# A Mamba-2 and MoBA trunk: the SSD inputs turned on VectorE, four head pairs to a visit, and an output block split in two

## The chip, the core and the metric

The kernel runs on one NeuronCore of one Trainium2 chip. The metric is the device time of one execution in microseconds; the time before is 1143.02 us, the median of three runs (1142.99 to 1146.43).

## What is computed

x is 256 tokens of 2048 float32 channels. A Mamba-2 layer with 64 heads of 64 channels in 8 groups is followed by an attention layer and a last RMSNorm. The change lies in the Mamba-2 layer:

```python
proj = h @ w_in                                   # z, xbc, dt
xbc = silu(causal_depthwise_conv(xbc, conv_w, conv_b))
dt = softplus(dt + dt_bias); a = dt * -exp(A_log)
x_dt = xs * dt[..., None]                         # xs: 8 groups x 8 heads x 64 channels
a_cum = cumsum(a); decay = exp(where(causal, a_cum[l] - a_cum[s], -inf))
cb = einsum("blgn,bsgn->blsg", cm, bm)
y = einsum("bsgrl,bsgrp->blgrp", cb * decay, x_dt)  # one chunk of 256 tokens: the state is zero
y = y + D_skip * xs
y = grouped_rmsnorm(y * silu(z), gnorm_g, 8)
x = x + y @ w_out                                 # 4096 rows of w_out, 512 to a group
```

## The kernel before

**The stream of products.** Nearly all of TensorE's work is weight matrices times activations. Each matrix is read as blocks of 512 columns; a *unit* is 256 rows of such a block. SyncE loads a unit into a `raw` buffer (512 KB, four of them), ScalarE rounds it to `hi`, VectorE makes the remainder `lo`, and TensorE does twelve products of 128x512 into two PSUM banks `ps` (two halves of the tokens, two slices of 128 rows, and hi, hi, lo). `hi` and `lo` have five buffers each, and the program writes the split of unit u+3 ahead of the products of unit u.

**The order of blocks** is the string ORDER: B and C are the columns of `bm` and `cm`, d those of dt, x0 to x7 and z0 to z7 the groups of `xs` and of the gate. o0 to o3 are four column blocks of `w_out` over groups 0 and 1, o10 to o13 the same columns over groups 2 and 3, p0 to p3 over groups 4 to 7 (eight units each). After them come the attention layer's matrices.

**Turning a block.** A finished block has tokens on the partitions and is wanted with channels there. `turn` has VectorE transpose 32x32 pieces into `T`, SyncE write `T` to DRAM (`turned`), and GpSimd's queue read it back in four pieces into `U`, in another order of the pieces.

**The side work.** The rest of the layer is written as generators, whose steps the program puts between the unit's products: `some` takes a step when a clock of its own, kept from costs for each instruction and DMA (LOAD, WRITE, READ), says that its inputs are there. That fixes each engine's order at build time; engines execute in that order and wait for data. For a group g these are:
- `conv_gen`: convolution and SiLU, giving `xs` (channels on the partitions). For x blocks it then transposes `xs` back on TensorE, two visits of four 128x128 transposes into a bank `s`; after each, VectorE multiplies by dt into `xd` (tokens on the partitions).
- `pair_gen`, four per group, one per pair of heads: loads the cumulated decay into `em` (two buffers), ScalarE and VectorE make `cb * decay`. Every second one then does the products of `xd` and `em` for two pairs, one bank for each, and VectorE adds the D term into `yt` and multiplies with the gate z.
- `norm_gen`: grouped RMSNorm, giving the operand `yn` of the o and p blocks.

All compute instructions have line 126 in the profile (a helper issues them), so rows are told apart by tile names.

Of the kernel before, what the change touches and what calls it, by code (L numbers as in the profile page):

```python
# [9 lines left out]
F32 = mybir.dt.float32  # L10
# [23 lines left out]
ORDER = "B0 d0 C0 x0 z0 x1 z1 x2 z2 x3 z3 B1 o0 C1 o1 x4 o2 z4 x5 o3 z5 x6 o10 z6 x7 o11 z7 o12 o13 p0 p1 p2 p3".split()  # L34
# [135 lines left out]
def trunk_kernel(ctx: ExitStack, tc: tile.TileContext, x, a_norm_g, a_w_in, a_conv_w, a_conv_b,  # L170
# [31 lines left out]
    def dram(t, offset, ap):  # L202
# [9 lines left out]
    S = [Slots(work, {"T": ([P, 512], 2), "u": ([P, 4, L], 1), "xs": ([P, 4, L], 3), "xd": ([P, 2, 512], 1),  # L212
                      "cb": ([P, 384], 4), "em": ([P, 2, 384], 2), "z": ([P, 1024], 1), "yt": ([P, 4, L], 2)})]
# [58 lines left out]
    def lay_out():  # L272
        for b in blocks:
            ks = b["ks"][::16 if b["form"] == "dt" else 2]
            if b["form"] == "rows":
                units.extend([(b, k, None) for k in ks[:3]] + [(b, k, j) for j in (0, 1) for k in ks[3:]])
            else:
                units.extend((b, k, None) for k in ks)

        def late(first, n, m):  # L280

            i = next(i for i, u in enumerate(units) if u[0] is first)
            p, q = units[i:i + n], units[i + n:i + 2 * n]
            units[i:i + 2 * n] = p[:n - m] + q[:n - m] + p[n - m:] + q[n - m:]

        late(blocks[n_out], 8, 2)
        late(blocks[n_fin], 8, 2)
# [121 lines left out]
    ga = const.tile([16, P], F32, name="ga")  # L409
# [90 lines left out]
    r0 = nt[:, 2, :]  # L500

# [6 lines left out]
    def first_norm():  # L508
        DVE.tensor_reduce(nt[:, 0, :], ss, axis=mybir.AxisListType.X, op=OP.add)
        root(nt, D)  # L510

# [65 lines left out]
    def dt_gen(w):  # L577
# [38 lines left out]
        dal = const.tile([P, 2, P], F32, name="dal", tag="c2")  # L616
# [4 lines left out]
    def conv_gen(U, there, c, key, group=None):  # L621
# [20 lines left out]
        give(u)  # L642
        st[key], when[key] = v, clock.last
        if group is None:
            return
        yield lambda: "dal" in st and can("xd")()
        xd = take("xd")
        for i in (0, 2):
            yield can("s")
            p = take("s").rearrange("p (t c) -> p t c", t=2)  # L650
            for e in range(2):
                for t in range(2):
                    PE.transpose(p[:, t, e * P:(e + 1) * P], v[:, i + e, t * P:(t + 1) * P], ident)
            yield
            h = 2 * (c + i)
            DVE.tensor_mul(xd[:, :, i * P:(i + 2) * P].rearrange("p t (h c) -> p t h c", h=4),
                           p.rearrange("p t (h c) -> p t h c", h=4),
                           st["dal"][:, :, h:h + 4, None].to_broadcast([P, 2, 4, 64]))
            give(p)
# [32 lines left out]
    def pair_gen(g, j):  # L692
# [17 lines left out]
        if j % 2:  # L710
            yield lambda: ("xd", g) in st and ("em", g, j - 1) in st
            yield max(when["xd", g], when["em", g, j - 1])
            yield lambda: of("s").free("s") > 1 and (("y", g) in st or can("yt")())
            for i in (j - 1, j):
                xd, E, q = st["xd", g], st.pop(("em", g, i)), take("s")[:, :L]
                for h in range(2):
                    PE.matmul(q[h * 64:(h + 1) * 64, :], lhsT=xd[:, 0, i * P + h * 64:i * P + (h + 1) * 64],
                              rhs=E[:, h, 0:256], start=True, stop=False)
                for h in range(2):
                    PE.matmul(q[h * 64:(h + 1) * 64, P:L], lhsT=xd[:, 1, i * P + h * 64:i * P + (h + 1) * 64],  # L720
                              rhs=E[:, h, 256:384], start=False, stop=True)
                give(E)
                st["q", g, i], when["q", g, i] = q, clock.last
            if ("y", g) not in st:
                st["y", g], st["n", g] = take("yt"), 0
            yield
        else:
            yield lambda: ("q", g, j) in st
            yield when["q", g, j]
        xd, xs, q = st["xd", g], st["xs", g], st.pop(("q", g, j))  # L730
        y = st["y", g][:, j, :]
        DVE.scalar_tensor_tensor(y, xs[:, j, :], Dv[:, c:c + 1], q, op0=OP.mult, op1=OP.add)
        give(q)
        st["x", g] = st.get(("x", g), 0) + 1
        if st["x", g] == 4:
            give(xs, xd, st["cb", g])
        yield lambda: ("z", g) in st
        z = st["z", g]
        y = y.rearrange("p (b l) -> p b l", l=32)
        DVE.scalar_tensor_tensor(y, y, 0.5, by_channel(z)[:, j], op0=OP.mult, op1=OP.mult)  # L740
        st["n", g] += 1
        if st["n", g] == 4 and g not in (1, 3):
            give(z)
# [39 lines left out]
    def z_gen(U, there, g):  # L783
# [8 lines left out]
        ACT.activation(z, U, AF.Tanh, scale=0.5)  # L792
# [5 lines left out]
    def z_evac(g):  # L798
        def evac(ps, t):
            U, there = turn(ps, t, r0)  # L800
# [4 lines left out]
    def x_evac(g):  # L805
        base = conv_evac(4 * g, ("xs", g), g)

        def evac(ps, t):
# [3 lines left out]
            for j in range(4):  # L812
                side.add(pair_gen(g, j), lambda: "AC" in st and can("em")())
# [69 lines left out]
    def r1_gen():  # L883
# [19 lines left out]
        csr = const.tile([P, 2, L], F32, name="csr", tag="c2")  # L903
# [16 lines left out]
    for name in ORDER:  # L920
# [262 lines left out]
    for u in range(len(units)):  # L1183
# [18 lines left out]
        if u == first_p + 12:  # L1202
            open_b()
# [44 lines left out]
```

## Time and profile before

| | before |
|---|---|
| median of three runs | 1143.02 us |
| the profiled execution | 1143.61 us, of which the span 1141.9 us |
| TensorE busy | 1130.1 us (99%) |
| VectorE busy | 839.2 us (73%) |
| ScalarE busy | 641.6 us (56%) |
| GpSimd busy | 124.4 us (11%) |
| TensorE in the chain that ended last | 96% |

The span runs from the first to the last instruction of the profiled execution; what its own time has beyond that lies around the program. The chain that ended last is followed back from the last instruction, at each step to what released it.

### The profile page before, as it was taken

To read this page: it belongs to the slowest core of one execution; us is meant where nothing else is said; L and a number is where in the kernel's file an instruction comes from. 1 tells how busy PE (TensorE), PEld (TensorE's weight loads), DVE (VectorE), ACT (ScalarE), POOL (GpSimd) and SP (SyncE) were. 2 spreads that over 40 slices of the span, in tenths; PEclk is the share of its full clock that TensorE was granted. 3 is DMA by queue.
4 is the path that set the end of the run, shared out by engine and by line. 5 is a ranking of instruction groups with operands and counts; after the bars stand their busy time and mean duration, and the time that the engine had idled before them with its cause. 6 is when DMAs were issued, how large, how long until landed. Compare 5 with 4: busy or idle time off the path is not lost.

```text
span 1141.9 us, 14900 instructions
## 1 busy us (share of the span) xinstructions
PE 1130.1 (99%) x5217; PEld 923.2 (81%) x5217; DVE 839.2 (73%) x1283; ACT 641.6 (56%) x890; POOL 124.4 (11%) x217
## 2 busy tenths in 40 slices
PE   9999999999999999999999999999999999999996
PEld 6888888888888888888878888888888888888885
DVE  5787878778799878787877558876445597887564
ACT  5666566767656666667554655434343444445353
POOL 2011112012011111101000000000000012122000
PEclk9999999999999999999999999999999999999998
DMA  8787888878778777777765467768658688888852
GB/s 263 222 242 242 249 229 278 268 243 253 210 222 240 223 237 225 237 234 231 215 232 177 162 197 218 224 200 261 220 174 244 209 248 237 263 250 261 254 185 92
DMA packets 130363, 258.91 MB, mean 227 GB/s; under 512 B 12976, under 2 KB 13824, under 8 KB 129904
## 3 DMA queue, kind: packets, MB, share of 16 engines
q1 hardware_dynamic: 119232, 226.01, 63.2%
q0 software_dynamic: 11056, 31.95, 10.9%
q8 instruction: 41, 0.67, 0.2%
q14 instruction: 34, 0.28, 0.1%
HBM read 235.83 MB, written 22.09 MB: 226 GB/s over the span
## 4 chain that ended last, share of the span: by engine, by line
PE 96%; DMA 1%; DVE 1%; ACT 0%; SPq 0%; issue 0%; ACTq 0%; DVEq 0%
PE ps L126 90%; PE s L126 6%; DMA raw<-in_a_w_in_dram 1%; PE ps_dt L126 0%; DVE xs L126 0%; DVE lo L126 0%; ACT hi L126 0%; SPq L416 0%; DVE x L126 0%; DVE T L126 0%; SPq L306 0%; ACT T L126 0%; ACT x L126 0%; DVE sfin L126 0%; ACTq L1243 0%
## 5 line engine op out<-in xcount | busy, mean ns | idle before, releaser
L126 DVE TENSOR_TENSOR lo<-raw,hi 128x1024 fp32r<-128x1024 f32 (+1 forms) x385 | 462.7, 1215 | 192.1 <-ACT hi L126 189.1
L126 ACT ACTIVATE hi<-raw 128x1024 fp32r<-128x1024 f32 (+1 forms) x385 | 397.7, 1052 | 263.3 <-PE ps L126 137.5
L126 PE MATMUL ps<-hi,hT 128*128 128x512 f32 x1280 | 401.1, 394 | 0.5 <-ACT hi L126 0.4
L126 PEld LDWEIGHTS ps<-hi,hT 128*128 128x128 f32 x1280 | 235.6, 188 | 49.2 <-issue 2.1
L126 PE MATMUL ps<-lo,hT 128*128 128x512 f32 x640 | 249.8, 390 | 0.0
L126 PE MATMUL ps<-hi,bop 128*128 128x512 f32 x512 | 161.1, 396 | 0.0
L126 PE MATMUL ps<-hi,yn 128*128 128x512 f32 x512 | 159.7, 393 | 0.0
L126 PE MATMUL ps<-hi,kvop 128*128 128x512 f32 x512 | 158.2, 390 | 0.0
L397 POOL DMA_DIRECT2D U<-turned x128 | 74.3, 587 | 748.9 <-DMA turned<-T 408.2
L126 PEld LDWEIGHTS ps<-lo,hT 128*128 128x128 f32 x640 | 120.1, 188 | 26.4 <-DVE lo L126 0.9
L126 PEld LDWEIGHTS ps<-hi,kvop 128*128 128x128 f32 x512 | 95.7, 188 | 19.7
L126 PEld LDWEIGHTS ps<-hi,bop 128*128 128x128 f32 x512 | 95.8, 188 | 19.4
L126 PEld LDWEIGHTS ps<-hi,yn 128*128 128x128 f32 x512 | 94.7, 188 | 19.4 <-issue 0.5
L126 PE MATMUL ps<-lo,yn 128*128 128x512 f32 x256 | 99.8, 390 | 0.0
L126 PE MATMUL ps<-lo,bop 128*128 128x512 f32 x256 | 99.8, 390 | 0.0
L126 PE MATMUL ps<-lo,kvop 128*128 128x512 f32 x256 | 99.7, 389 | 0.0
L126 PE MATMUL ps<-hi,oop 128*128 128x512 f32 x256 | 78.9, 390 | 0.0
L126 DVE STREAM_TRANSPOSE T<-ps 128x512 f32<-128x512 f32 x64 | 43.4, 699 | 25.6 <-ACT ps L126 15.9
L126 DVE SCALAR_TENSOR_TENSOR xs<-u,cw,xs 128x255 f32<-128x255 f32 (+2 forms) x144 | 59.7, 475 | 0.0
L126 ACT ACTIVATE em<-em,dal 128x128 f32<-128x128 f32 (+1 forms) x128 | 54.4, 449 | 5.0 <-DMA em<-AC 2.9
L126 PEld LDWEIGHTS ps<-lo,bop 128*128 128x128 f32 x256 | 48.0, 188 | 10.3
L126 PEld LDWEIGHTS ps<-lo,yn 128*128 128x128 f32 x256 | 48.0, 188 | 10.1
(165 smaller groups left out, 922.5 us busy)
## 6 DMA issues: line engine op xcount, KB each, us to landing
raw<-in_a_w_in_dram SPq DMA_DIRECT2D x159, 512.0 KB, 5.3
raw<-in_a_w_out_dram SPq DMA_DIRECT2D x64, 512.0 KB, 4.8
raw<-in_w_kv_dram SPq DMA_DIRECT2D x64, 512.0 KB, 4.8
raw<-in_b_w_in_dram SPq DMA_DIRECT2D x64, 512.0 KB, 4.7
turned<-T SPq DMA_DIRECT2D x64, 256.0 KB, 4.3
U<-turned POOLq DMA_DIRECT2D x128, 128.0 KB, 6.5
raw<-in_b_w_out_dram SPq DMA_DIRECT2D x32, 512.0 KB, 4.9
em<-AC POOLq DMA_DIRECT2D x32, 256.0 KB, 6.0
```

The costliest lines, as they stand in the source:

```text
L126: return call(out, *args, **kw)
L397: POOL.dma_start(U[32 * q:32 * q + 32].rearrange("p (b c) -> p b c", b=8), src)
```

## The change

For an x block, `conv_gen` no longer transposes on TensorE. VectorE transposes `xs` in 32x32 pieces into the buffer `u` (two instructions), SyncE writes `u` to DRAM (`turned_x`), GpSimd's queue reads it back into `u` in four pieces, and VectorE multiplies by dt into `xd` in four instructions. `u` (one buffer) is held until then. `pair_gen` becomes `em_gen`, which ends with `cb * decay`; a new `y_gen` per group does the products of all four pairs in one visit, two pairs to a bank, adds the D term in place in `xs`, and multiplies with z two pairs at a time. `em` has four buffers instead of two, `xs` four instead of three, and `yt` is gone. The factor 0.5 of the gate moves into the row factor `r0h` of the z blocks. Blocks p0 to p3 now cover groups 6 and 7 (four units each), and new blocks o20 to o23 ahead of them cover groups 4 and 5.

```diff
-ORDER = "... z6 x7 o11 z7 o12 o13 p0 p1 p2 p3".split()
+ORDER = "... z6 x7 o11 z7 o12 o13 o20 o21 o22 o23 p0 p1 p2 p3".split()
...
-"u": ([P, 4, L], 1), "xs": ([P, 4, L], 3), "em": ([P, 2, 384], 2), "yt": ([P, 4, L], 2)
+"u": ([P, 4, L], 1), "xs": ([P, 4, L], 4), "em": ([P, 2, 384], 4)
...
         DVE.scalar_tensor_tensor(v, u, 1.0, v, op0=OP.add, op1=OP.mult)
-        give(u)
         st[key], when[key] = v, clock.last
         if group is None:
+            give(u)
             return
+        yield
+        U = u.rearrange("p j l -> p (j l)")
+        for t in range(2):
+            DVE.transpose(U.rearrange("p (b t j l) -> p t b j l", b=4, t=2, j=4)[:, t],
+                          v[:, :, t * P:(t + 1) * P].rearrange("p j (b l) -> p b j l", b=4))
+        X = hbm.tile([P, 1024], F32, name="turned_x", tag=f"X{group % 2}")
+        SP.dma_start(X, U)
+        written = DVE.ns + WRITE
+        for b in range(4):
+            src = bass.AP(tensor=X.tensor, offset=X.offset + b * L, ap=[[1024, 32], [32 * 1024, 4], [1, L]])
+            POOL.dma_start(U[32 * b:32 * b + 32].rearrange("p (a c) -> p a c", a=4), src)
+        yield copied(U, written, 4 * 600.0)
         yield lambda: "dal" in st and can("xd")()
         xd = take("xd")
-        for i in (0, 2):
-            yield can("s")
-            p = take("s").rearrange("p (t c) -> p t c", t=2)
-            for e in range(2):
-                for t in range(2):
-                    PE.transpose(p[:, t, e * P:(e + 1) * P], v[:, i + e, t * P:(t + 1) * P], ident)
-            yield
-            h = 2 * (c + i)
-            DVE.tensor_mul(xd[:, :, i * P:(i + 2) * P] ..., p ..., st["dal"][:, :, h:h + 4, None] ...)
-            give(p)
+        for t in range(2):
+            for h in range(2):
+                DVE.tensor_mul(xd[:, t] ..., U ..., st["dal"][:, t, 2 * c + h:2 * c + h + 8:2] ...)
+        give(u)
...
+    def y_gen(g):
+        yield lambda: ("xd", g) in st and st.get(("ems", g)) == 4
+        yield max(when["xd", g], *(when["em", g, j] for j in range(4)))
+        yield lambda: of("s").free("s") > 1
+        xd, y = st["xd", g], st["xs", g]
+        Q = []
+        for i in (0, 2):
+            q = take("s").rearrange("p (j l) -> p j l", j=2)
+            Q.append(q)
+            for j in (i, i + 1):
+                E = st.pop(("em", g, j))
+                ...                                  # the four products of a pair, as before
+        give(xd)
+        for i in (0, 2):
+            yield
+            for j in (i, i + 1):
+                c = 4 * g + j
+                DVE.scalar_tensor_tensor(y[:, j, :], y[:, j, :], Dv[:, c:c + 1], Q[i // 2][:, j - i, :], ...)
+            give(Q[i // 2])
+        yield lambda: ("z", g) in st
+        z = st["z", g]
+        for i in (0, 2):
+            DVE.tensor_mul(v, v, by_channel(z)[:, i:i + 2])      # v: pairs i and i + 1 of y
+            yield
...
-            ks = range(8 * (i // 10), 8 * (i // 10) + 8) if kind == "o" else range(16, 32)
+            ks = range(8 * (i // 10), 8 * (i // 10) + 8) if kind == "o" else range(24, 32)
```

Three places show what the engines' orders become. The first is TensorE in the block z1, after group 0's `xs` is there, before the change (`ident,xs` are the transposes back, `em,xd` the products of two pairs; `x4` is the count):

```order
L126 MATMUL ps<-lo,hT 128x512
L126 MATMUL s<-ident,xs 128x128 x4
L126 MATMUL ps<-hi,hT 128x512 x2
...
L126 MATMUL ps<-lo,hT 128x512
L126 MATMUL s<-em,xd 64x256 x2
L126 MATMUL s<-em,xd 64x128 x2
L126 MATMUL s<-em,xd 64x256 x2
L126 MATMUL s<-em,xd 64x128 x2
L126 MATMUL ps<-hi,hT 128x512 x2
```

The products of group 0 in the changed kernel, on TensorE, now in block x2:

```order
L126 MATMUL ps<-lo,hT 128x512
L126 MATMUL s<-em,xd 64x256 x2
L126 MATMUL s<-em,xd 64x128 x2
L126 MATMUL s<-em,xd 64x256 x2
L126 MATMUL s<-em,xd 64x128 x2
L126 MATMUL s<-em,xd 64x256 x2
L126 MATMUL s<-em,xd 64x128 x2
L126 MATMUL s<-em,xd 64x256 x2
L126 MATMUL s<-em,xd 64x128 x2
L126 MATMUL ps<-hi,hT 128x512 x2
```

The transposes are gone (all 64 of them over the eight groups; the other counts of TensorE's instructions are the same), and the products of four pairs stand together, behind `xd` and all four `em`.

The second place is VectorE between the two halves of block x1 (the `T` rows with `cb` between them) and group 0's `xd`, before:

```order
L126 STREAM_TRANSPOSE T<-ps 128x512
L126 TENSOR_TENSOR lo<-raw,hi 128x1024 x2
L126 TENSOR_TENSOR xd<-s,dal 128x2x256
L126 SCALAR_TENSOR_TENSOR z<-z,U 128x1024
L126 TENSOR_TENSOR lo<-raw,hi 128x1024
L126 TENSOR_TENSOR xd<-s,dal 128x2x256
L126 TENSOR_TENSOR lo<-raw,hi 128x1024
L126 SCALAR_TENSOR_TENSOR yt<-xs,Dv,s 128x256
```

and in the changed kernel from the transposes into `u` on, which follow the same `T` row and one `lo` (`xs<-u,cw` are the convolution of the next group, `xs<-xs,Dv` the D term of group 0):

```order
L126 STREAM_TRANSPOSE u<-xs 128x4x128 x2
...
L126 SCALAR_TENSOR_TENSOR z<-z,U 128x1024
L126 TENSOR_TENSOR lo<-raw,hi 128x1024 x2
L126 STREAM_TRANSPOSE T<-ps 128x512
L126 TENSOR_TENSOR xd<-u,dal 128x4x64 x4
L126 STREAM_TRANSPOSE T<-ps 128x512
L126 TENSOR_TENSOR lo<-raw,hi 128x1024 x2
L126 SCALAR_TENSOR_TENSOR xs<-u,cw,xs 128x255 x4
L126 SCALAR_TENSOR_TENSOR xs<-u,cw,xs 128x254 x4
L126 SCALAR_TENSOR_TENSOR xs<-xs,Dv,s 128x256 x2
L126 TENSOR_TENSOR lo<-raw,hi 128x1024
```

Between the transposes into `u` and the `xd` rows that read it back stand the `lo` rows of seven units; in the other groups it is seven (groups 3 and 4), eight (1 and 5) or six (2, 6 and 7). The next group's convolution, which needs `u` too, starts behind `xd`, and two of its steps and half of group 0's D term stand between the same two `lo` rows.

The third place is GpSimd's queue in the same stretch, where `-` is before and `+` the changed kernel:

```order
 L397 DMA U<-turned 32x8x128 x4
-L698 DMA em<-AC 128x2x256 x2
+L706 DMA em<-AC 128x2x256 x4
 L397 DMA U<-turned 32x8x128 x8
-L698 DMA em<-AC 128x2x256 x2
+L658 DMA u<-turned_x 32x4x256 x4
 L397 DMA U<-turned 32x8x128 x4
-L698 DMA em<-AC 128x2x256 x2
+L706 DMA em<-AC 128x2x256 x4
+L658 DMA u<-turned_x 32x4x256 x4
```

The reads into `u` of groups 0 and 1 stand behind the `U` reads of later blocks and, for group 1, behind four `em` loads whose buffers come free when group 0's products have been done.

## Rows read from the trace of the kernel before

**Rows 1.** The page, parts 1 and 2: busy time, and granted clock by slices.
```profile
PE 1130.1 (99%) x5217; PEld 923.2 (81%) x5217; DVE 839.2 (73%) x1283; ACT 641.6 (56%) x890; POOL 124.4 (11%) x217
...
PEclk9999999999999999999999999999999999999998
```

**Rows 2.** The waits, TensorE alone: total us, times, longest us.
```profile
PE s L126 <- DVE early L126: 1.2, 1, 1.2
PE s L126 <- DMA xl<-in_x_dram: 0.5, 1, 0.5
PE ps L126 <- ACT hi L126: 0.4, 1, 0.4
```

**Rows 3.** The waits, all engines (same columns).
```profile
ACT hi L126 <- PE ps L126: 137.5, 93, 3.0
...
ACT u L126 <- DMA U<-turned: 6.5, 4, 3.2
...
ACT z L126 <- DMA U<-turned: 5.3, 3, 4.8
```

**Rows 4.** Timeline, TensorE, 101 to 144 us: start, us, operation, count.
```profile
102.09 0.39 PE L126 MATMUL ps<-lo,hT 128*128 128x512 f32 x1
...
109.57 0.39 PE L126 MATMUL ps<-lo,hT 128*128 128x512 f32 x1
...
132.01 0.39 PE L126 MATMUL ps<-lo,hT 128*128 128x512 f32 x1
132.24 0.60 PE L126 MATMUL s<-ident,xs 128*128 128x128 f32 x4
...
136.58 0.39 PE L126 MATMUL ps<-lo,hT 128*128 128x512 f32 x1
...
139.76 0.39 PE L126 MATMUL ps<-lo,hT 128*128 128x512 f32 x1
140.08 1.52 PE L126 MATMUL s<-em,xd 128*64 128x256 f32 x16
141.53 0.73 PE L126 MATMUL ps<-hi,hT 128*128 128x512 f32 x2
...
143.48 0.39 PE L126 MATMUL ps<-lo,hT 128*128 128x512 f32 x1
```

**Rows 5.** TensorE by form: count, busy us, mean ns.
```profile
L126 PE MATMUL s<-ident,xs 128*128 128x128 f32 x64 | 9.6, 272 | 0.0
```

**Rows 6.** VectorE by form: count, busy us, mean ns.
```profile
L126 DVE TENSOR_TENSOR lo<-raw,hi 128x1024 fp32r<-128x1024 f32 x383 | 461.3, 1218 | 191.5 <-ACT hi L126 188.5 <-PE ps L126 2.0
L126 DVE STREAM_TRANSPOSE T<-ps 128x512 f32<-128x512 f32 x64 | 43.4, 699 | 25.6 <-ACT ps L126 15.9 <-DMA turned<-T 5.0 <-PE ps L126 4.6
...
L126 DVE TENSOR_TENSOR x<-ps,x 128x512 f32<-128x512 f32 x32 | 21.5, 686 | 18.4 <-PE ps L126 18.4
L126 DVE SCALAR_TENSOR_TENSOR xs<-u,cw,xs 128x255 f32<-128x255 f32 x48 | 19.9, 477 | 0.0
...
L126 DVE SCALAR_TENSOR_TENSOR yt<-yt,z 128x256 f32<-128x256 f32 x32 | 13.1, 419 | 0.2
...
L126 DVE TENSOR_TENSOR xd<-s,dal 128x512 f32<-128x512 f32 x16 | 10.9, 683 | 0.1
```

**Rows 7.** DMA issues by line: count, KB each, median us to landing.
```profile
raw<-in_a_w_in_dram SPq DMA_DIRECT2D x159, 512.0 KB, 5.3
...
turned<-T SPq DMA_DIRECT2D x64, 256.0 KB, 4.3
U<-turned POOLq DMA_DIRECT2D x128, 128.0 KB, 6.5
```

**Rows 8.** Tile U: duration of its issues, and its landing times.
```profile
L397 POOL DMA_DIRECT2D U<-turned x128: 582/585/610, 43.3 to 1049.8; - x128
...
DMA to landing us min/median/max: 2.7/6.5/8.8
```

**Rows 9.** Windows: busy us (instructions) per engine, clock, DMA share, GB/s.
```profile
100.00:200.00 100.00, 100.00 (x482) 81.52 (x481) 77.04 (x117) 65.72 (x88) 14.70 (x24) 1.00 0.85 250
```

More of the change, by code (lines that the diff above doesn't have):

```diff
@@ L31 @@
 MARGIN = 750.0
-ORDER = "B0 d0 C0 x0 z0 x1 z1 x2 z2 x3 z3 B1 o0 C1 o1 x4 o2 z4 x5 o3 z5 x6 o10 z6 x7 o11 z7 o12 o13 p0 p1 p2 p3".split()
+ORDER = "B0 d0 C0 x0 z0 x1 z1 x2 z2 x3 z3 B1 o0 C1 o1 x4 o2 z4 x5 o3 z5 x6 o10 z6 x7 o11 z7 o12 o13 o20 o21 o22 o23 p0 p1 p2 p3".split()
 LOAD = 4700.0
@@ L284, in late @@
             units[i:i + 2 * n] = p[:n - m] + q[:n - m] + p[n - m:] + q[n - m:]
-        late(blocks[n_out], 8, 2)
+        late(blocks[n_out], 4, 2)
         late(blocks[n_fin], 8, 2)
@@ L500, in trunk_kernel @@
     r0 = nt[:, 2, :]
+    r0h = const.tile([P, 2], F32, name="r0h")
     def squares(h):
@@ L510, in first_norm @@
         root(nt, D)
+        DVE.tensor_scalar(r0h, r0, 0.5, None, op0=OP.mult)
     gv = const.tile([P, 112], F32, name="gv")
@@ L690, in c_evac, with em_gen @@
         return evac
-    def pair_gen(g, j):
+    def em_gen(g, j):
         c = 4 * g + j
@@ L709, in pair_gen @@
         st["em", g, j], when["em", g, j] = E, clock.last
[L710 to L715, printed above, removed]
+        st["ems", g] = st.get(("ems", g), 0) + 1
+        if st["ems", g] == 4:
+            give(st["cb", g])
@@ L718, in pair_gen @@
                               rhs=E[:, h, 0:256], start=True, stop=False)
                 for h in range(2):
-                    PE.matmul(q[h * 64:(h + 1) * 64, P:L], lhsT=xd[:, 1, i * P + h * 64:i * P + (h + 1) * 64],
+                    PE.matmul(q[h * 64:(h + 1) * 64, j - i, P:L], lhsT=xd[:, 1, j * P + h * 64:j * P + (h + 1) * 64],
                               rhs=E[:, h, 256:384], start=False, stop=True)
                 give(E)
-                st["q", g, i], when["q", g, i] = q, clock.last
@@ L724, in pair_gen @@
-            if ("y", g) not in st:
-                st["y", g], st["n", g] = take("yt"), 0
+        give(xd)
+        for i in (0, 2):
             yield
[L727 to L734, printed above, removed]
@@ L735, in pair_gen @@
-        if st["x", g] == 4:
-            give(xs, xd, st["cb", g])
+            for j in (i, i + 1):
+                c = 4 * g + j
+                DVE.scalar_tensor_tensor(y[:, j, :], y[:, j, :], Dv[:, c:c + 1], Q[i // 2][:, j - i, :],
+                                         op0=OP.mult, op1=OP.add)
+            give(Q[i // 2])
         yield lambda: ("z", g) in st
         z = st["z", g]
-        y = y.rearrange("p (b l) -> p b l", l=32)
-        DVE.scalar_tensor_tensor(y, y, 0.5, by_channel(z)[:, j], op0=OP.mult, op1=OP.mult)
@@ L741, in pair_gen @@
-        st["n", g] += 1
-        if st["n", g] == 4 and g not in (1, 3):
+        for i in (0, 2):
+            v = y[:, i:i + 2, :].rearrange("p j (b l) -> p j b l", l=32)
+            DVE.tensor_mul(v, v, by_channel(z)[:, i:i + 2])
+            yield
+        st["y", g] = y
+        st["n", g] = 4
+        if g not in (1, 3):
             give(z)
@@ L799, in evac @@
         def evac(ps, t):
-            U, there = turn(ps, t, r0)
+            U, there = turn(ps, t, r0h)
             if t:
@@ L812, in evac @@
             for j in range(4):
-                side.add(pair_gen(g, j), lambda: "AC" in st and can("em")())
+                side.add(em_gen(g, j), lambda: "AC" in st and can("em")())
+            side.add(y_gen(g))
             side.add(norm_gen(g), lambda: st.get(("n", g)) == 4)
@@ L1201, in trunk_kernel @@
             force(lambda: need in st)
-        if u == first_p + 12:
+        if u == first_p + 4:
             open_b()
```

20 lines of the change are left out of this document (10 added, 10 removed).

## The prediction

> **What bounds the kernel now.** I read the page first, then the waits of TensorE, then its timeline. The page gives TensorE 99% of the span at a granted clock that shows 9 tenths or more (the digit for 90% and up) in all slices but the last [rows 1]. A busy share near 99% could hide pipelined instructions, so I looked at what TensorE waited for: 1.2, 0.5 and 0.4 us, 2.1 us in all, in the whole execution [rows 2]. The other side of it is that ScalarE, which makes `hi`, waits 93 times and 137.5 us for TensorE to give a buffer back [rows 3]: the supply runs ahead and the products hold it up. Last, the timeline gives the pace: from the start at 102.09 to the one at 109.57 lie 33 products in 7.48 us, 0.2267 us each, and nothing else [rows 4]. At that pace a unit of twelve is 2.72 us. So the time is the sum of what TensorE is given to do, and the other engines count only when they make it wait.
>
> **The transposes that go.** 64 transposes leave TensorE [rows 5], in 16 visits of four. Their 9.6 us of busy time overlaps neighbours and is not their price. The price is read start to start: from the `lo` product at 132.01 to that at 136.58 there are 18 products and one visit; 4.57 less 18 times 0.2267 leaves 0.49 us. From 136.58 to 139.76 there are 12 products and one visit: 3.18 less 2.72 leaves 0.46 us [rows 4]. I take 0.475; 16 of them are 7.6 us (7.4 to 7.8). TensorE had no slack to lose it in, so all of it is on the path.
>
> A rule of the Trainium skill speaks against this edit. The page "VectorE: DVE Perf Modes", sections "The three transpose paths" and "Rules for kernel authors", advises TensorE for a 128x128 transpose where PSUM will do, and puts one at 390 ns on TensorE against 311 ns on VectorE, which only turns 32x32 blocks. By its figure the 64 would be 25 us, an estimate from that page alone; the visits above show a third of that and decide the sum.
>
> **Four pairs to a visit.** The products of `xd` and `em` stay the same in number, but come in 8 visits instead of 16. From 139.76 to 143.48 there are 9 products and one visit: 3.72 less 2.04 is 1.68 us, of which 1.45 us lie between the visit's first start and the next product's [rows 4]. The difference, 0.23 us, is what entering and leaving costs, if it does not grow with the visit. Eight visits fewer save 1.8 us; the bounds are 0 (if the 0.23 us belongs to each pair) and 1.8.
>
> **What VectorE gets.** Per group it gains two transposes of 512 (0.699 us, as `T`), four multiplications of 256 for `xd` and two of 512 with the gate, and loses two of 512 from PSUM (0.683 us) and four of 256 with the gate (0.419 us) [rows 6]. The new `xd` form is not in the trace; its width is that of the 0.419 us row, its neighbours in kind 0.68 us, and I take 0.42 since the width sets those rows. So 1.40 + 4 x 0.42 + 2 x 0.68 less 1.37 and 1.68 is 1.4 us per group, 11 us over eight; at 0.68 it would be 19 us. The four new blocks o20 to o23 add eight additions of 0.686 us, 5.5 us [rows 6]. Between 100 and 200 us VectorE is busy 77.0 of 100 us [rows 9], so 17 us over the some 600 us of this stage are hidden by idle time; on TensorE the split of p into o2 and p adds nothing, since its products are counted alike. If that cover were gone, the 17 us would come through whole. Scaling z by `r0h` replaces a factor and costs one tiny instruction.
>
> **What the queues get.** Eight writes of 512 KB on SyncE and 32 reads of 128 KB on GpSimd's queue: 1 MB more in each group. DMA is 0.85 busy between 100 and 200 us [rows 9]. SyncE's loads behind the write are for `raw` buffers that VectorE must free first, so standing behind it costs nothing while the four buffers last: a load lands 5.3 us after issue [rows 7] and the buffer is wanted four units, 10.9 us, later. On GpSimd's queue the reads are 32 issues of 0.585 us [rows 8], 19 us in a queue that works 14.7 of 100 us [rows 9]. `em` with four buffers lets its loads go earlier, which moves work but adds none.
>
> **The new wait.** `xd` now waits on VectorE for a round trip, and behind it in the same engine stand the turning of the next block and the `lo` of the next units; behind those, and behind `xd` itself in the visit of four pairs, TensorE. The trip by its rows is a write of 4.3 us (for half the bytes), four issues, 2.3 us, and 6.5 us to land [rows 7, 8]: 13.1 us, 15.4 with the slowest landing of 8.8. The order leaves six to eight units, 16.3 to 21.8 us. That fits, but the same kind of trip for `U` was late before: `u` waited four times in its 12, `z` three in its 8, 11.8 us together [rows 3], that is 7 of 20 and 1.7 us each. Eight trips at that rate make VectorE wait 8 x 7/20 x 1.7 = 4.8 us. How much reaches TensorE the trace can't show: before, none of the 11.8 us did [rows 2], which is the lower bound, and 4.8 us, all of it, is the upper one. I take 1.0, nearer to the lower bound, because the splits stand three units ahead, while the visit itself stands closer to `xd` than any product did to `U`.
>
> **The sum.** The profiled execution took 1143.6 us. Less 7.6, less 1.8, plus 1.0 is 1135.2; its own time lies 0.6 us above the median of the runs shown, so I say 1134.6 us, 0.7% less.
>
> **The rivals.**
>
> *The trips are late in every group (slower).* If DMA, with 1 MB more per group at 0.85 busy, makes each trip late by the 1.7 us that `U` missed by on average, and TensorE waits as long in each visit, the eight groups cost 13.6 us: 1143.0 - 9.4 + 13.6 = 1147.2 us. It decides from 1.2 us per group on, where 9.4 us are used up. For it speaks that the new buffer `u` is single, so that the next group's convolution is held up too; against it that the room is 3 us and more over the trip. Chance 0.08.
>
> *VectorE bunches.* `u` is held longer, so the next convolution starts late and its steps crowd: behind group 0's `xd` stand eight steps of 0.477 us and two D terms between two `lo` rows, 4.8 us, where a unit leaves 2.72 - 1.22 = 1.5 us [rows 6]. That is 3.3 us behind in one go. The lead of three units, 8.2 us, swallows it once, but not if the engine is already late. If half of it reaches TensorE in three groups, 5 us come back: 1139.6 us. Chance 0.14.
>
> *TensorE was not the bound.* Then its shorter work leaves the time as it is, 1143.0, or what the 2.1 us of waits grow to. The Trainium skill would make this more likely than I do: "Trace Analysis", section "Identifying the Most-Contended Engine", calls matmul busy time no good measure and takes the busy share of weight loads, which is 81% here [rows 1], so a fifth would be free. The unbroken pace of 0.2267 us and the waits of 2.1 us say that products follow each other without a gap. Chance 0.04.
>
> **How the numbers follow.** The forecast has 0.74. Its own range is 1133.4 (7.8 and 1.8 us saved, no stall) to 1139.3 us (7.6 and half of 1.8 saved, all 4.8 us come through). A measurement of this kernel tells some 0.3%, 3.4 us, from no change, so faster means under 1139.6. Half of the bunching case lies below that: faster 0.81, within 0.07 + 0.04 = 0.11, slower 0.08. The range to hold 8 in 10 takes the forecast's own range, most of the bunching case, and at the low end the 2.1 us of waits that might vanish: 1131.0 to 1141.0 us.
>
> **What would show it.** In the changed kernel's trace: no transposes of `xs` on TensorE; eight visits of 32 records each about 3.1 us from product to product (2 x 1.45 + 0.23); TensorE's waits still a few us in all, with any growth put down to `xd`, `u` or `hi` and `lo`; 1.4 us more of VectorE per group. The prediction is wrong if TensorE waits more than 6 us for these, or if the pace of 0.2267 us changes.

## The result, and the profile after

The changed kernel takes 1157.83 us (median of four runs, 1152.61 to 1159.60), the kernel before 1143.01 us (1142.72 to 1146.43). The ratio is 1.0116, with a 95% interval of 1.0097 to 1.0135: slower by 1.2%, where 0.7% faster was forecast. The profiled execution took 1158.28 us.

The page of the changed kernel, busy times and slices (answers to [rows 1]):

```profile
PE 1128.9 (98%) x5153; PEld 923.6 (80%) x5153; DVE 850.4 (74%) x1308; ACT 639.0 (55%) x890; POOL 142.3 (12%) x249
...
PE   9999998999999999999999989999999999999996
```

TensorE is still at 98%, but the row of slices has 8s in it, where before only the last slice was below 9. What it waited for (engine, tile, releaser: us in all, times, longest; answers to [rows 2]):

```profile
PE s L126 <- ACT hi L126: 3.8, 2, 1.9
PE s L126 <- issue: 3.2, 1, 3.2
PE s L126 <- DVE x L126: 3.2, 3, 2.2
PE s L126 <- DVE r L126: 2.3, 1, 2.3
PE s L126 <- DVE xs L126: 2.3, 1, 2.3
PE s L126 <- DVE early L126: 1.2, 1, 1.2
```

These rows give 16.0 us where all rows gave 2.1. Two things are to be seen. All of it is waited by tiles `s`, the small visits between products; the products themselves wait for almost nothing (0.7 us). And no row names `xd`, but that does not mean that TensorE never waits for it. The row `issue`, and a smaller one put down to `ps` (0.8 us in two), are visits of `em` and `xd`: those of groups 1, 0 and 4, at 201.99, 158.80 and 428.33 us. Each starts 0.1 us after the first `xd` multiplication of its group ends on VectorE. So TensorE waits 4.0 us for `xd`, and the stretch below shows why. VectorE's own wait for the round trip of x is one row, and small, as is the wait of `u` for `U` (all engines, 100 to 640 us; [rows 3] for before):

```profile
ACT u L126 <- DMA U<-turned: 7.9, 2, 4.9
...
DVE xd L126 <- DMA u<-turned_x: 1.4, 2, 1.1
```

To see where the time went, I laid the two traces side by side by unit of twelve products: the start of the first `lo` product of unit n, changed kernel minus kernel before. Each column is one execution. The four other columns belong to versions told below.

| unit | before, us | changed | e1 | e5 | g1 | g4 |
|---|---|---|---|---|---|---|
| 24 | 83.09 | -0.90 | -0.65 | -0.52 | -0.06 | +0.26 |
| 34 | 112.28 | +2.87 | +0.80 | +0.26 | +1.16 | +0.55 |
| 64 | 202.62 | +11.36 | +6.53 | +1.82 | +5.58 | +2.68 |
| 192 | 582.40 | +3.20 | -0.45 | -7.25 | -4.35 | -8.40 |
| 200 | 606.08 | +4.51 | +9.04 | +1.44 | -2.73 | -6.85 |
| 216 | 651.88 | +3.01 | +8.80 | +1.16 | -2.73 | -6.85 |
| 232 | 697.68 | +12.67 | +8.80 | +1.16 | -2.73 | -6.85 |
| 383 | 1130.08 | +14.67 | +12.19 | +4.47 | -0.29 | -4.27 |

The column of the changed kernel has four stretches. Up to unit 64 it loses 11.4 us net. From 64 to 216 it gains 8.4 us, where the forecast's share for these six groups is 6/8 of 9.4, 7.0 us; some 1.5 us of the 8.4 come of the unit chosen, since one of the two visits of group 1 lies behind unit 64 in the kernel before (226.06 us) and ahead of it in the changed one. From 216 to 232 it loses 9.7 us, and 2.0 us later on.

A column is one execution, and the early loss differs between executions: e1, in which VectorE and ScalarE have the changed kernel's order up to 590 us, is at +6.53 at unit 64. The 3.8 us between units 24 and 34 lie ahead of the first trip (its write goes out at 136.72 us), so they are not the trip's own.

**The first stretch.** Windows of the changed kernel, a long one and two short ones (us, busy time and count by engine, granted clock, DMA share, GB/s); [rows 9] has DMA at 0.85 and 250 GB/s between 100 and 200 us:

```profile
100.00:200.00 100.00, 95.67 (x434) 77.98 (x434) 71.60 (x99) 64.65 (x93) 16.94 (x29) 0.98 0.92 270
...
190.00:200.00 10.00, 8.75 (x39) 6.92 (x37) 5.61 (x9) 5.36 (x9) 1.63 (x3) 1.00 0.93 315
200.00:210.00 10.00, 8.01 (x43) 6.79 (x44) 8.47 (x21) 4.23 (x5) 2.16 (x4) 0.66 0.98 292
```

Landing times on the page are hardly longer for the weights (5.4 us where [rows 7] has 5.3) and for `U` (6.6 after 6.5); `em` takes 7.9 us, and 6.0 before. The time shows in what ScalarE waits for between 100 and 640 us. The first fence is the kernel before, the second the changed one, both with the rows for weights alone:

```profile
ACT hi L126 <- DMA raw<-in_a_w_in_dram: 33.4, 19, 3.8
...
ACT hi L126 <- DMA raw<-in_a_w_out_dram: 11.1, 3, 4.0
```

```profile
ACT hi L126 <- DMA raw<-in_a_w_in_dram: 45.8, 23, 5.1
...
ACT hi L126 <- DMA raw<-in_a_w_out_dram: 13.2, 9, 3.5
```

44.5 us before, 59.0 us after. This wait differs between executions too (e2, which has the order of the kernel before in this stretch, gives 30.2 us), so here are the same two rows of the other traces, summed: the versions with all eight trips at full size have 53.7 us (g1) to 70.8 us (h1), those without any trip 30.2 us (e2) to 45.6 us (e5), those with fewer trips or fewer bytes 36.0 to 49.3 us.

Weights come later, `hi` and `lo` with them, and what stands behind `lo` on VectorE too. The visit of group 1 shows it, ScalarE first and then VectorE:

```profile
196.57 1.06 ACT L126 ACTIVATE hi<-raw 128x1024 fp32r<-128x1024 f32 x1 [2.98 <-DMA raw<-in_a_w_in_dram]
```

```profile
197.67 1.23 DVE L126 TENSOR_TENSOR lo<-raw,hi 128x1024 fp32r<-128x1024 f32 x1 [4.30 <-ACT hi L126]
...
200.26 1.23 DVE L126 TENSOR_TENSOR lo<-raw,hi 128x1024 fp32r<-128x1024 f32 x1 [0.35 <-ACT hi L126]
...
201.47 1.43 DVE L126 TENSOR_TENSOR xd<-u,dal 128x256 f32<-128x256 f32 x4
```

The trip of this group had landed at 187.3 us. Its `xd` comes 14 us later because it stands behind two `lo`, which wait for `hi`, which waits for weights (2.98 us, then 1.53 us). TensorE's products still have three units in hand, but the visit has not: it starts at 201.99 us, 3.63 us after the product ahead of it.

**The third stretch** lies where the out products end and the x1 steps begin. TensorE and VectorE in the changed kernel's timeline:

```profile
680.67 0.38 PE L126 MATMUL s<-ident,x 128*128 128x128 f32 x2
683.26 0.30 PE L126 MATMUL s<-ident,x 128*128 128x128 f32 x1 [2.21 <-DVE x L126]
684.16 0.33 PE L126 MATMUL s<-ident,x 128*128 128x128 f32 x1 [0.60 <-DVE x L126]
```

```profile
681.28 1.22 DVE L126 TENSOR_TENSOR lo<-raw,hi 128x1024 fp32r<-128x1024 f32 x1 [1.40 <-ACT hi L126]
682.43 0.68 DVE L126 TENSOR_TENSOR x<-ps,x 128x512 f32<-128x512 f32 x1
683.03 0.48 DVE L126 SCALAR_TENSOR_TENSOR kvop<-s,gv,kvop 128x256 fp32r<-128x256 f32 x1
683.42 0.68 DVE L126 TENSOR_TENSOR x<-ps,x 128x512 f32<-128x512 f32 x1
```

The last p block is done before 679.30, where the `kvop` products start, yet VectorE adds it to x only at 682.43, behind a `lo` that itself waits 1.40 us for ScalarE; TensorE stands with its transposes of x at 680.67 and gets the second half 2.6 and 3.5 us later.

### The profile page after: what moved, and what is told of

Read it like the earlier page. It is cut to its first block, busy times and chain, and to the rows that moved or that the text cites. A ratio compares the mean times of both kernels' runs of the same rounds, so it can differ in the third digit from the quotient of the medians.

```text
span 1156.5 us, 14856 instructions
## 1 busy us (share of the span) xinstructions
PE 1128.9 (98%) x5153; PEld 923.6 (80%) x5153; DVE 850.4 (74%) x1308; ACT 639.0 (55%) x890; POOL 142.3 (12%) x249
## 4 chain that ended last, share of the span: by engine, by line
PE 72%; DMA 10%; DVE 8%; ACT 4%; issue 4%; POOL 1%; SPq 0%; ACTq 0%; DVEq 0%; POOLq 0%
PE ps L126 68%; PE s L126 4%; DVE lo L126 3%; DMA U<-turned 3%; DMA raw<-in_a_w_in_dram 3%; ACT hi L126 2%; DMA Es<-turned_E 1%; DMA turned<-T 1%; DVE xs L126 1%; DMA turned_E<-PT 1%; DVE T L126 1%; DMA raw<-in_b_w_in_dram 1%; POOL U L397 1%; DVE Es L126 0%; POOL Es L1052 0%
## 5 line engine op out<-in xcount | busy, mean ns | idle before, releaser
L126 PEld LDWEIGHTS ps<-hi,hT 128*128 128x128 f32 x1280 | 238.0, 189 | 49.8 <-issue 1.2
L126 PEld LDWEIGHTS ps<-lo,kvop 128*128 128x128 f32 x256 | 48.5, 189 | 11.0 <-DVE lo L126 0.9
```

What stands on the lines that cost most here:

```text
L126: return call(out, *args, **kw)
```

## The experiments

Each version was timed beside the kernel before on the same chip, where the latter's medians lay between 1143.1 and 1144.1 us; a ratio is to that. "e1", "g1" and so on stand for the full names. I began with two losses in mind, an early one from the round trips and a late one from the split.

**e1_no_split: the out products in the old order.**

```diff
-... z7 o12 o13 o20 o21 o22 o23 p0 p1 p2 p3
+... z7 o12 o13 p0 p1 p2 p3
-            ks = ... else range(24, 32)
+            ks = ... else range(16, 32)
```

(Two counts that go with the order, for the layout of the p blocks and the unit at which the next stage opens, go back with it.)

> The changed kernel with the out products in the old order (p with all sixteen k of groups 4 to 7, no o20 to o23), all else as changed. Theory A (two separate losses: one of some 9.5 us where the x1 steps follow the short p blocks between 660 and 697 us, one of some 14 us between 98 and 210 us from x turned on VectorE): 1157.8 less 9.5, 1148 us, and no start-to-start gap over 0.9 us left after 640 us. Theory B (everything lost is lost to the round trips of x, and the gaps after 640 us only follow from them): within 2 us of 1157.8. Theory C (the split costs its 5.5 us of additions on VectorE): 1152.

1156.5 us, 1.0104 [1.0081, 1.0126]. Theory A's place was right and its price wrong. The gaps at the x1 steps are gone (+8.80 at units 216 and 232), but as much is lost earlier, between units 192 and 200. TensorE there:

```profile
600.73 0.50 PE L126 MATMUL ps<-hi,yn 128*128 128x512 f32 x1 [3.73 <-ACT yn L126]
601.99 0.80 PE L126 MATMUL ps<-hi,yn 128*128 128x512 f32 x1 [0.76 <-DVE yn L126]
```

The old p blocks want the normed y of group 6 at unit 197, and with x turned by way of memory it is not ready: VectorE makes D terms, then the norm's multiplications from 597.94, then ScalarE and VectorE make the two parts of `yn`. So the split and the late y belong together: the split gives the y of groups 6 and 7 twelve and eight units more, and pays for it at x1.

**e2_split_alone: the kernel before with the split alone** (the lines of e1 the other way round).

> The kernel before with only the out products split (o20 to o23 and p of eight k). Theory A: 1143.0 plus 9.5, 1152 us, with the gaps of TensorE between 660 and 700 us and none before. Theory B: 1143.0 within 1 us. Theory C: 1148.5.

1150.2 us, 1.0062 [1.0044, 1.0079]. The split by itself costs 6.8 us, at the place named: its TensorE waits, all of them in one answer, are

```profile
PE s L126 <- DVE x L126: 3.2, 3, 2.2
PE s L126 <- DVE early L126: 1.2, 1, 1.2
PE s L126 <- DVE r L126: 0.9, 1, 0.9
```

with the same 3.2 us for x as in the changed kernel. The waits are 4.1 us without `early`; the rest is TensorE after them, where six products start between 678.69 and 680.97, 0.46 us apart, not 0.2267: the granted clock of that stretch is 0.50, the lower level of 1.2 GHz. Theory C's 5.5 us of additions was near in size and wrong in kind: VectorE is idle again and again there.

**e3_x_on_tensor: e1 with x turned on TensorE, four pairs to a visit kept.**

```diff
-        X = hbm.tile(...); SP.dma_start(X, U); four POOL.dma_start(U[...], src)
+        for i in (0, 2): four PE.transpose(...), one DVE.tensor_mul(xd[...], p, dal)
```

> e1_no_split with x turned on TensorE again, so with no round trip of x, but with four pairs to a visit, four em buffers and y in place. Theory A1 (the early loss comes from the round trip of x, by its wait or its traffic): 1143.0 less 1.8 for the fewer visits, 1141 us, with no gaps between 98 and 210 us. Theory A2 (it comes from the visit of four pairs: four em loads at once, and two banks taken together): e1_no_split plus the 7.6 us of the transposes, 1153 to 1156 us.

1150.0 us, 1.0058 [1.0038, 1.0077]. Between A1 and A2, so neither is the whole: without round trips 6.5 us of e1's come back though 7.6 us of transposes return, but 7 us over the kernel before stay.

**e4_no_wait: e1, but xd doesn't wait for the trip.**

```diff
-                               U.rearrange("p (h a t j c) -> p h t j a c", ...)
+                               v.rearrange("p j l -> p (j l)").rearrange(...)
```

> e1_no_split, but xd is multiplied from xs as it stands before the turning, so that it doesn't wait for the round trip (xd and all that follows from it are other numbers). The write, the four reads, the turning on VectorE and the order of every engine stay as in e1_no_split. If the wait of xd for the trip makes the early loss: 1134 to 1137 us. If the traffic of the trip (weights that land later) or the crowd on VectorE makes it: as e1_no_split within 2 us. Half way would say both.

1153.6 us, 1.0085 [1.0058, 1.0112]; the interval holds e1's ratio. The landing of the trip is at most a small part of the loss (2.9 us by the medians). The visits are late all the same: those of groups 0, 1, 5 and 7 take 9.0 us more in all than unpaused ones, as three take 8.1 us more in the changed kernel, for `xd` stands behind the same `lo`.

**e5_no_traffic: e1 without the transfers of the trip.**

```diff
-        SP.dma_start(X, U)
-        for b in range(4): POOL.dma_start(U[32 * b:32 * b + 32]..., src)
```

> e1_no_split without the write of the turned x and its four reads, so xd is multiplied from blocks that stand in the wrong places (other numbers); the order on TensorE, VectorE and ScalarE is that of e1_no_split row by row. Theory T (1 MB more per group makes the weights land late between 140 and 210 us): the 9 us that e1_no_split loses there go, 1147 to 1149 us. Theory V (VectorE and ScalarE are crowded by the order, with or without traffic): 1153 to 1157 us, with the gaps before the norm's transposes as in e1_no_split.

1145.6 us, 1.0017 [1.0004, 1.0030]: 10.9 us less than e1, with the same order on the three engines. Theory T, with the reserve that the wait for the landing is gone too (2.9 us by e4's median). ScalarE's wait for weights between 100 and 640 us falls back to 45.6 us, as before the change:

```profile
ACT hi L126 <- DMA raw<-in_a_w_in_dram: 39.6, 23, 3.8
...
ACT hi L126 <- DMA raw<-in_a_w_out_dram: 6.0, 5, 2.7
```

In the table, e5 is at +1.82 at unit 64 where e1 is at +6.53; the stall at unit 197 stays. So does a part of the early one: the visits of groups 1 and 4 take 2 us more each than unpaused ones, without any trip. That part is the order's.

**e6_traffic_on_tensor: the transfers without their use.** e3 with a write of `xs` as it stands and the four reads, into a buffer that nobody reads.

> e3_x_on_tensor (x turned on TensorE, four pairs to a visit) with the write of 512 KB and the four reads of 128 KB per group added, into the buffer u that nobody reads. Theory T: e3_x_on_tensor plus about 9 us, 1158 us. Theory V: 1150 to 1152 us.

1167.2 us, 1.0202 [1.0183, 1.0221]: 17.2 us more than e3, more than T expected. But e6 is not e3 plus transfers alone. The order of VectorE and ScalarE differs from e3's, and the reads hold `u`, which the next convolution needs: ScalarE waits 32.1 us at `u` for them or for what stands ahead of them in GpSimd's queue (once 12.5 us), against 2.2 us in the changed kernel. How much of the 17.2 us that makes is not shown.

**e7_two_visits: e3 with two visits per group.**

```diff
-        yield lambda: ("xd", g) in st and st.get(("ems", g)) == 4
+        for i in (0, 2):
+            yield lambda: ("em", g, i) in st and ("em", g, i + 1) in st
```

> e3_x_on_tensor with the products of xd and em in two visits of two pairs per group as before, each as soon as its two em are there, but still four em buffers whose loads go out together, and y in place. If one visit of four pairs is what costs e3_x_on_tensor its 7 us (D terms, gates and squares come at once, and the norm's transposes wait for VectorE): 1143 to 1145 us. If it is the four em made together, which hold up hi on ScalarE, or the changed buffers: 1149 to 1152 us.

1147.7 us, 1.0043 [1.0027, 1.0059], between the two answers; with e3's interval overlapping it tells little.

**e9_middle_groups: the kernel before, x on VectorE in groups 2 to 6 alone.**

```diff
+        if group in (0, 1, 7):
             ... four PE.transpose(...) twice, as before
+        else:
+            ... DVE.transpose, write, four reads, xd from U
```

> The kernel before with x turned on VectorE, by way of the round trip, for groups 2 to 6 alone; groups 0, 1 and 7 turn it on TensorE, and visits of two pairs, buffers and order of blocks are as before. Forty transposes leave TensorE, 5 x 0.95 = 4.75 us. If the trip costs time only where DMA is full (groups 0, 1) and where the last group's yn is awaited: 1143.0 less 4.75, 1138 us. If the trip eats its savings in any group: 1143 us or more.

1158.0 us, 1.0116 [1.0100, 1.0133]. A miss by 20 us, but its trace is plain: at unit 152 it is 4.7 us ahead of the kernel before, the 4.75 us forecast, and at 192 still 3.5 us; between units 200 and 208 it loses 15 us, where the squares and the norm of group 7 come at unit 204, not at 199.75.

**f1_groups_2_5 and f2_groups_1_5: other groups.** As e9, with `if group in (0, 1, 6, 7)` and `(0, 6, 7)`.

> As e9_middle_groups, but group 6 too turns x on TensorE, so VectorE and the round trip serve groups 2 to 5 alone; by the order, the last norm's transposes of group 7 come at unit 199.25 as in the kernel before (199.75), not at 204. If the 15 us that e9_middle_groups lost after unit 192 are the late yn of groups 6 and 7: they go, and 4 x 0.95 = 3.8 us stay saved: 1139 to 1141 us. If they are a cost of the trips that would turn up elsewhere: over 1145 us.

> As f1_groups_2_5, with group 1 too on VectorE. If group 1 with its full DMA (180 to 220 us) can't carry a trip: 3 us or more slower than f1_groups_2_5. If a trip costs only where yn is awaited: 0.95 us faster, 1138 to 1140 us.

1155.3 us, 1.0096 [1.0077, 1.0114], and 1183.6 us, 1.0348 [1.0321, 1.0375]. Both expectations failed. f1 moved the stall from group 7 to group 6: one wait of 6.7 us for `yn`, 11 us lost between units 192 and 200. In f2 the stall comes earlier: its longest wait is 13.5 us for VectorE's `em` at 276 us, in block o0, which wants the y of group 1. The `em` are made from loads that go out at 278.62 us, in GpSimd's queue behind reads of `U` that had waited 19.1 us; so this one is not a late y by itself, and that the early call for the y of group 1 put things in this order was not tried. I had looked at one group's place in the order. In e9 and in f1 the late y is that of the first group behind those with trips, 7 and 6, which itself turns x on TensorE, so the trips seem to put off what stands behind them too.

**f3_volume_only and f4_waits_only: bytes or waits.** e6 with the reads taken from the input x, so that they wait for no write; and e6 with an eighth of the bytes and the same waits.

```diff
-            src = ...(tensor=X.tensor, offset=X.offset + b * L, ap=[[1024, 32], ...])
+            src = ...(tensor=x.tensor, offset=x.offset + b * L, ap=[[D, 32], ...])
```

```diff
-        SP.dma_start(X, v.rearrange("p j l -> p (j l)"))
+        SP.dma_start(X[:, 0:P], v[:, 0, 0:P])
...
```

> e6_traffic_on_tensor with the four reads of 128 KB per group taken from the input x, so that they wait for no write to land; bytes, issues and order of instructions on all queues stay. If the bytes make the 17 us of e6_traffic_on_tensor: 1165 to 1168 us. If GpSimd's queue makes them, where the reads of em and U stand behind the wait for the write: 1150 to 1153 us.

> e6_traffic_on_tensor with a write of 64 KB and four reads of 16 KB in place of 512 KB and 128 KB: the same issues, the same order and the same waits for the landing of the write, an eighth of the bytes. If the bytes make the 17 us: 1150 to 1154 us. If the waits in the queues do: 1160 us or more.

1172.3 us, 1.0246 [1.0220, 1.0271], and 1159.9 us, 1.0145 [1.0119, 1.0171]. f3 is no faster than e6: the wait for the write in GpSimd's queue costs nothing that shows. f4 is 7.3 us faster than e6 and 9.9 us slower than e3. The order of VectorE and ScalarE is the same in e6, f3 and f4, so bytes make about 7 of e6's 17 us; the other 10 come with the eight writes, the 32 reads, the longer hold of the buffer and the order that differs from e3's, and these were not taken apart.

**g1_no_split_yn: e1 with y of group 6 wanted four units later.**

```diff
         late(blocks[n_out], 8, 2)
+        late(blocks[n_out], 6, 2)
```

> e1_no_split with one line more: the blocks p0 and p1 are laid out so that the products with yn of group 6 come four units later (at unit 201, not 197), those with group 7 where they were; the same number of products. If the 9.5 us that e1_no_split loses at 597 us are TensorE waiting for the late yn of group 6: they go, 1147 us, with no gap over 1 us between 580 and 620 us. If the lateness only moves on to the yn of group 7 or into the x1 steps: 1152 us or more.

1150.3 us, 1.0065 [1.0049, 1.0080], runs from 1143.6 to 1153.1: 6.2 us less than e1. Windows of e1, then of g1, around the place:

```profile
580.00:600.00 20.00, 16.29 (x90) 12.66 (x88) 16.86 (x31) 7.59 (x8) 3.83 (x7) 1.00 0.87 265
600.00:620.00 20.00, 18.52 (x76) 14.92 (x77) 15.28 (x30) 8.94 (x9) 0.00 (x0) 0.91 0.35 118
```

```profile
580.00:600.00 20.00, 20.00 (x110) 16.43 (x109) 17.41 (x30) 8.21 (x9) 1.09 (x2) 1.00 0.75 217
600.00:620.00 20.00, 20.00 (x92) 16.50 (x91) 15.01 (x30) 8.90 (x9) 0.00 (x0) 1.00 0.62 210
```

The stall is gone, and nothing takes its place at x1 (-2.73 at units 200 to 232). The profiled execution is g1's fastest, so its column is a few us better than its median.

**g2_tensor_017 and g3_pairs_017:** g1 with groups 0, 1 and 7 on TensorE, and e9 with g1's line.

> g1_no_split_yn with groups 0, 1 and 7 turned on TensorE: VectorE and the round trip for groups 2 to 6, four pairs to a visit. If the early 9 us are those of the two trips that fall where DMA is full (140 to 210 us), they go too, at the price of 3 x 0.95 = 2.9 us of transposes: 1140 to 1142 us. If any trip costs more than it saves: 1146 us or more.

> e9_middle_groups with the same one line: visits of two pairs, groups 2 to 6 on VectorE. e9_middle_groups had 3.5 us saved at unit 192 and lost 17 us after it. If the late yn is all of that loss: 1140 to 1142 us. The yn of group 7 still stands later in the order than it is wanted (unit 205); if its wait stays, 1143 to 1150 us.

1149.6 us, 1.0048 [1.0033, 1.0064], and 1155.8 us, 1.0103 [1.0090, 1.0116]. g2 is as g1: the three trips that it saves are worth their 2.9 us of transposes and no more, so the first groups' trips are not the dear ones, or others became so; its TensorE waits are now for the norm's squares (3.9 us in three). g3 keeps the wait for group 7's y, the second branch of its expectation, only dearer (15 us between units 200 and 208).

**g4_no_traffic_yn: e5 with g1's line**, so with neither named loss.

> e5_no_traffic (no write and no reads of the turned x, other numbers) with the same one line. Both named losses are gone then, so if they are the whole of what the prediction missed, its 9.4 us come out: 1134 to 1138 us. If something else of the change costs time (visits of four pairs, four em at once): 1140 us or more.

1137.7 us, 0.9952 [0.9938, 0.9967]: 5.5 us faster than the kernel before, and 12.6 us faster than g1, which has the same order and the transfers. Its page and its longest waits of TensorE:

```profile
PE 1121.8 (99%) x5153; PEld 919.6 (81%) x5153; DVE 846.5 (74%) x1300; ACT 640.9 (56%) x890; POOL 124.7 (11%) x217
```

```profile
PE s L126 <- issue: 1.7, 1, 1.7
PE s L126 <- DVE early L126: 1.2, 1, 1.2
PE s L126 <- DMA Es<-turned_E: 1.1, 1, 1.1
PE ps L126 <- DVE lo L126: 1.0, 1, 1.0
```

At unit 192 it is 8.40 us ahead. TensorE's saving is real; it is the transfers and the late y that the saving was paid with. The kernel leaves out the turning by way of memory, so it shows a price and is no way to get the saving.

**h1_x_load_later and h2_before_x_later: other bytes out of the same stretch.** g1, and the kernel before, with

```diff
-    side.add(x1_load(), lambda: st.get(("n", 0)) == 4)
+    side.add(x1_load(), lambda: st.get(("n", 1)) == 4)
```

> g1_no_split_yn with the load of x (two of 1 MB on GpSimd's queue) sent after group 1's y instead of group 0's; on TensorE, VectorE and ScalarE the order stays but for one pair of rows on VectorE. If the bytes between 140 and 210 us make the early loss, 2 MB less there (some 7 us of DMA at the 286 to 314 GB/s of that stretch) give 3 to 7 us back: 1144 to 1147 us. If the crowd on VectorE makes it: 1150 us.

> The kernel before with the same change of the load of x alone. Its TensorE waits for nothing there, so by either theory 1143 us; its order of the side work shifts a little, which may cost up to 2 us.

1152.3 us, 1.0083 [1.0070, 1.0097], and 1143.4 us, 1.0003 [0.9993, 1.0012]. Moving 2 MB that are not the trip's gave nothing back: GB/s between 180 and 200 us fell from 314 to 246, and h1 is still 5.15 us behind at unit 64. So it is not simply the number of bytes in that stretch; ScalarE's wait for weights, over 100 to 640 us, did not fall either (70.8 us).

Of the versions that leave nothing out, none came out faster than the kernel before.

## Why the prediction was wrong

**What bounds the kernel: right.** The pace of a product stayed 0.2267 us where TensorE had not just waited, and g4, with less work for TensorE, is faster, which a TensorE that was not the bound would not give.

**The transposes: right.** No `ident,xs` row is left. The 390 ns that the prediction takes from the Trainium skill ("VectorE: DVE Perf Modes", section "The three transpose paths") stand there for bfloat16, and these blocks are float32. The advice there, TensorE for such a transpose, fits the outcome, but by the price of the round trip, which the sum has at 1.0 us. **Four pairs to a visit: right, and worth more than forecast.** Read as the prediction read its 1.68 us, an unpaused visit of the changed kernel costs 2.97 us: from the `lo` at 276.34 to the one at 279.99 there are three products and the visit, 3.65 less 0.68 us. Two visits before were 3.36 us, so a group saves 0.39 us, not 0.23: 3.1 us over eight groups. The two together show between units 64 and 216, and in g4's 8.4 us at unit 192.

**VectorE: right that it is hidden in the sum, and its size smaller than forecast.** It works 850.4 us, 11.2 us more, not 16.5. The new form of `xd` takes 418 ns, the 0.42 taken:

```profile
L126 DVE TENSOR_TENSOR xd<-u,dal 128x256 f32<-128x256 f32 x32 | 11.4, 418 | 1.4 <-DMA u<-turned_x 1.4
```

**The new wait: the path right, its cause and its size wrong.** VectorE waits 1.4 us for the trips, not 4.8, and e4 shows their landing to be worth little. But TensorE waits 4.0 us for `xd` in the changed kernel's trace, where the sum has 1.0, and the three visits that wait take 8.1 us more than unpaused ones. With the rows for `hi` and `lo` that is 8.5 us, over the 6 us that the prediction named as its sign of being wrong. What makes `xd` late is not the trip ahead of it but the `lo` ahead of it on VectorE, which wait for weights. The rival of late trips came nearest in time (1147.2) and was wrong in kind: in six of eight groups the trip had landed before VectorE came to `xd`. Of the rival in which VectorE bunches, a part is there: with the same order and no transfers the visits still lose 4.1 us (e5) and 2.3 us (g4).

**What the queues get: the first step that failed.** The prediction gave the trip's transfers no term in the sum: "standing behind it costs nothing while the four buffers last" and "moves work but adds none" are the sentences. The transfers cost 10.9 us (e5 against e1) and 12.6 us (g4 against g1); some 2.9 us of the first may be the wait for their landing (e4). I had priced each queue by its own issues and had asked only whether the new reader waits for its data. But the loads of weights share the core's 16 DMA engines with the trip. The row for DMA, 0.85 busy, is a mean; a window of the kernel before that I read only afterwards has stretches with nothing left:

```profile
190.00:200.00 10.00, 10.00 (x55) 7.75 (x55) 8.87 (x23) 3.56 (x4) 1.43 (x2) 1.00 1.02 324
```

TensorE lost nothing there before. With the trips ScalarE's wait for weights grew by 14.5 us; what was behind it on VectorE moved, and TensorE met it at its visits. How it divides between bytes, number of transfers and the hold of `u` is not settled: in f4 an eighth of the bytes still goes with 9.9 us over e3, though not by the transfers alone, and in h1 2 MB fewer of other bytes gave nothing back.

**The split: the second step that failed.** The sentence is "on TensorE the split of p into o2 and p adds nothing, since its products are counted alike". The count is alike, but the p blocks are now four units, 10.9 us, and each is followed by x1 steps of VectorE, ScalarE and TensorE in turn that were spread over eight. They run into each other and into the `kvop` products: 6.8 us alone (e2), 9.7 us in the changed kernel's trace. In the other direction the prediction missed what the split is worth: without it the later y of group 6 stalls TensorE, 6.2 us (e1 against g1) and 7.9 us (e5 against g4). The question "what is late next" was asked of the next product, not of the next block that wants this y.

**The sum by the runs:** 1143 less 9.4, plus about 12 for the transfers, plus 7 to 10 for the split or the late y, is 1153 to 1156 us; measured 1157.8. Some 2 to 5 us stay open, and 1.3 us more with the 3.1 us that the visits really save. g4 has such a rest too: 1137.7, where 1143.2 less 9.4 would be 1133.8; its visit of group 1 makes 2.3 us of it. In e3 and e7, which have no round trip, 4 to 7 us are over; part of it falls after 640 us (2.7 us between units 256 and 272 and 4.6 us after 336 in e3). There TensorE waits 2.1 us for `lo` and, at 1073 us, 2.5 us for the landing of `Es`, after which the granted clock is 0.50 for 3.4 us; the kernel before has neither wait. Why they come was not tried.

## What to carry to other kernels

A transfer is priced by what shares the DMA engines with it, in the stretch where it falls, and not only by whether its own reader waits: where DMA is as busy as here (0.85 on the mean, 1.02 in a stretch) and weights stream, look who waits for weights, and what stands behind that one on its engine. A row of waits that does not name a tile does not clear it: compare the start of the visit with the end of what it reads. When a step is made later by a round trip, follow its result to the block that wants it, and see how many units are left there. Equal counts of products are not equal schedules: a shorter block brings its epilogue into the next one.

## What the runs showed of the hardware

A wait costs TensorE more than its length. The visit of four pairs takes 2.75 us when TensorE comes to it without a pause (five of the eight in the changed kernel). After a pause of 3.63 us (start to start) it took twice that:

```profile
198.36 0.39 PE L126 MATMUL ps<-lo,hT 128*128 128x512 f32 x1
201.99 5.67 PE L126 MATMUL s<-em,xd 128*64 128x256 f32 x32 [3.24 <-issue]
207.59 0.85 PE L126 MATMUL ps<-hi,hT 128*128 128x512 f32 x2
```

The granted clock was at its lower level, 1.2 GHz and not 2.4, over the whole of this visit (windows as above):

```profile
200.00:201.00 1.00, 0.00 (x0) 0.00 (x0) 0.74 (x1) 0.65 (x2) 0.72 (x2) 1.00 0.77 191
201.10:207.80 6.70, 5.81 (x33) 5.00 (x34) 6.46 (x19) 3.48 (x4) 1.44 (x2) 0.50 1.02 293
207.90:210.00 2.10, 2.10 (x11) 1.70 (x11) 1.07 (x3) 0.00 (x0) 0.00 (x0) 1.00 0.96 337
```

The clock fell near the end of the pause, and half the clock goes with twice the time. It was 0.50 also from 102.1 to 105.4 us, after the wait of 2.26 us, and from 699.4 to 702.8 us, after one of 2.33 us; products start some 0.43 us apart there. Not every wait of such length is followed by it: after the one of 2.21 us at 683 us the clock stayed at 1.00.

After pauses of 0.80 and 0.73 us (at 158.00 and 427.60) the same visit took 3.3 us, with the clock at 1.00. There the other three `xd` multiplications of the group were still running when the visit had begun (up to 159.70 us in the first), so it may have waited inside; that is not shown.

Of the 11.4 us lost by unit 64, about 5 us come on top of the waits' lengths: 1.6 us of slower products after the wait at 98 us, 0.5 us in the visit at 158 us and 2.9 us in that at 202 us. The prediction counted waits by their length alone.
